# Branches A and B of a gated decoder block: GpSimd joins the turned halves, nine heads of A divide on VectorE, the products with V stand later

## The chip, the cores and the metric

The kernel runs on one NeuronCore of a Trainium2 chip. A core has TensorE (PE, matrix products into PSUM), VectorE (DVE), ScalarE (ACT), GpSimd (POOL) and SyncE (SP, which here only issues DMAs). Each engine works through its own queue in order; semaphores hold an instruction until what it reads or overwrites is ready. The metric is device time of one execution in microseconds (us). The profile adds a record of one execution: start and length of every instruction, and the clock that TensorE was granted.

## The reference

One decoder layer on 512 tokens of width 2048. A normed input is projected once and split over three token mixers, whose outputs are gated, projected, weighted and summed. Only the parts that the change touches are shown:

```python
def sliding_window_attention(...):          # branch A: 12 query heads, 4 key heads of 64
    scores = einsum('bnqkgd,bnskd->bnkgqs', qb, kb) * (d ** -0.5)
    scores = where(valid, scores + bias, NEG)            # ALiBi; each block sees itself and the one before
    m = maximum(max(scores, -1), sink)
    p = exp(scores - m)
    denom = sum(p, -1) + exp(sink - m)
    out = einsum('bnkgqs,bnskd->bnqkgd', p / denom, vb)

def forgetting_attention(...):              # branch B: 12 heads of 64
    sc = einsum('bqhd,bshd->bhqs', qb, k) * scale + cq - ck     # causal
    out = einsum('bhqs,bshd->bqhd', softmax(where(mask, sc, NEG)), v)

def hybrid_layer(...):
    proj = rms_norm(x) @ w_in
    ua = (ya * silu(za)) @ w_branch_a;  ub = ...;  uc = ...
    y = g[0] * ua + g[1] * ub + g[2] * uc
    return x + y @ w_out
```

All inputs are 32-bit floats.

## The kernel before

A 32-bit number enters TensorE as two parts: a rounded one (`hi`, an ACT copy) and the rest (`lo`, a DVE subtraction). Each large product is three: hi by hi, hi by lo, lo by hi.

**The main stream.** The input projection runs as chunks: `qB0, kB0, vB0, qB1, kB1, vB1, qA0, qA1, kvA, z0, mem, qC, z1, z2, z3`. A chunk is eight units (`mem`: sixteen smaller ones); a unit loads two 128-row slices of the weights (SP), splits them (ACT line 212, DVE line 215) and multiplies (PE line 301). A unit is 24 main products on PE (`mem`: 12): 384 columns wide in the B and A chunks, 512 from `kvA` on. After a chunk's last unit four PSUM banks are emptied (line 446 for queries and keys, lines 464 and 466 for values). After `z3` come the gate logits, branch products and output product; the change touches nothing there.

**The order of the work.** All of it is written by hand. A clock counts main products: three of them are half a step unit (`tick`), so a *step unit* below is six main products. Each attention head is a `Chain`: a base time and a list of steps with offsets (`STEPS_B`, `STEPS_A`), and named counters that hold a step back until a buffer is free in the planned order. At each tick the steps that are due are written into the engines' queues between the main products. So the step numbers say where an instruction stands in its queue, not when it runs. Branch B's heads 0 to 5 run under `qB1, kB1, vB1`, heads 6 to 11 under `qA0, qA1, kvA`; branch A's twelve heads run under `z0, mem, qC`; branch C's after them.

**One head of B** (A alike, with other offsets and sizes): GpSimd makes the bias (lines 625, 626); PE makes the scores of four 128-query blocks (589, 590); DVE adds the bias and finds the maximum (613); ACT takes the exponential and its sum (616); DVE inverts the sum (593) and the block is divided by it (594: on DVE for B, on GpSimd for A). The probabilities must then be turned, keys on the partitions. That goes by DMA in 16-bit halves:

- *halves* (636, 638; A: 724, 726, 728): GpSimd sorts the upper and lower 16 bits of each number apart, into `s1`;
- *send* (643; A: 734): SP issues one transposing DMA, `s1` to `s2`;
- *join* (649; A: 739): the halves are put together again into 32-bit numbers, `pt`. 2560 16-bit elements per partition in B, 1792 in A; read in order, written with a gap;
- *hi* (655; A: 745) on ACT, then *lo* (658; A: 748) on DVE;
- *products with V* (667; A: 757): eight on PE, which alternate between hi and lo; then ACT and DVE copy the result out (579, 583).

`PH`, `PL`, `pt`, `s1` and `s2` exist once each, so each waits for its last reader.

`STEPS_B[10..14]` are send, join, hi, lo, products; `STEPS_A[4], [5], [6], [10], [11]` the same for A. `scaled` (line 592) holds the reciprocal and the division.

Of the kernel before, what the change touches and what calls it, by code (L numbers as in the profile page):

```python
# [31 lines left out]
UK = 2  # L32
BOFF = (0, 512, 1024, 896)

BASES_B = ((14, 26, 38, 46, 58, 70), (14, 26, 38, 46, 58, 70))
BASES_A = (10, 18, 26, 34, 42, 50, 62, 69, 76, 83, 90, 97)
BASES_C = (12.0, 19.5, 28.0, 33.5)
STEPS_B = (-12, -8.5, -2, -1.5, 0, 1, 1.0, 1.5, 3.5, 5, 10.5, 16.5, 18, 19, 20.5, 4.5)
STEPS_A = (-5.0, -1.0, -0.5, -1.5, 6.5, 10.5, 11.5, -6.5, 3, 3.5, 12.5, 13.5)
STEPS_C = (-8, -3.5, 0.5, 1, 8.0, 4.5, 10)  # L40

PREP_Q = ((-1.5, 22.0, 43.5), (2.5, 22.0, 43.5))
# [8 lines left out]
EXP_B, EXP_A, EXP_C, DIV_B, DIV_A, DIV_C = (1.0, 0.5, 1.0, 3, 3.5, 3.0)  # L51
# [6 lines left out]
def tile_hybrid_block(ctx, tc, xT, x, memT, mem, ng, mng, w_in, b_forget, gqa, gka, sinks, gqb, gkb, gqc, gkc,  # L58
                      w_mem, w_a, w_b, w_c, w_out, relm, out):
    nc = tc.nc  # L60
    ve, ac, po, pe, sy = nc.vector, nc.scalar, nc.gpsimd, nc.tensor, nc.sync
# [7 lines left out]
    def f32(ap):  # L69
        return ap.bitcast(F32)  # L70
# [68 lines left out]
    def at_slot(t, f):  # L139

        heapq.heappush(agenda, (t, next(seq), f))

    def later(dt, f):
        at_slot(clock[0] + dt, f)
# [246 lines left out]
    def u16(ap):  # L391
        return ap.bitcast(U16)
# [142 lines left out]
    def sbank(name):  # L535
        return bank(1, name)
# [55 lines left out]
    def scaled(p, den, i, engine=po):  # L592
        ve.reciprocal(den[:, 4 + i:5 + i], den[:, i:i + 1])  # L593
        engine.tensor_scalar(p, p, den[:, 4 + i:5 + i], None, op0=ALU.mult)  # L594

    def head_B(h, kv):

        s = {}

        def s1(i):  # L600
            q, kh, kl, v, hv, cb = kv()
            if i == 0:
                s["p"] = at.p.tile([P, 1280], F32, tag="P", bufs=2, name=f"pB{h}")
                s["den"] = cp.tile([P, 16], F32, tag="den", bufs=2, name=f"denB{h}")
            p, den = s["p"], s["den"]
            o = (0, 128, 384, 768)[i]
            n = (i + 1) * P
            bi = s["b", i]
            sb = sbank(f"sB{h}_{i}")
            scores(sb[:, :n], q, kh, kl, i, slice(0, n))  # L610
            pi = p[:, o:o + n]
            nm = den[:, 8 + i:9 + i]
            ve.tensor_tensor_reduce(out=pi, in0=sb[:, :n], in1=bi[:, :n], scale=-1.0, scalar=3.0e38,  # L613
                                    op0=ALU.add, op1=ALU.min, accum_out=nm)
            release("bias")
            later(EXP_B, lambda: ac.activation(pi, pi, AF.Exp, bias=nm, scale=-1.0, accum_out=den[:, i:i + 1]))  # L616
            later(DIV_B, lambda: scaled(pi, den, i, ve))
            s["p", i] = pi
            if i > 1:
                later(DIV_B + 0.5, lambda: halves(i))  # L620

        def sb(i):
            n = (i + 1) * P
            bi = at.p.tile([P, S], F32, tag="bias", bufs=2, name=f"biB{h}_{i}")
            po.tensor_scalar(bi[:, :n], kv()[5][:, :n], -1.0, cq[:, i, h:h + 1], op0=ALU.mult, op1=ALU.add)
            po.affine_select(out=bi[:, i * P:n], in_=bi[:, i * P:n], pattern=[[-1, P]], compare_op=ALU.is_ge,
                             fill=NEG, base=0, channel_multiplier=1)
            s["b", i] = bi

        def halves(i):  # L630

            if i == 0:
                s["s1"] = spare(0, f"s1B{h}", U16, 2560).rearrange("p (e j n) -> p e j n", e=2, n=P)
            src = u16(s["p", i]).rearrange("p (j n e) -> p e j n", n=P, e=2)
            n = min(i + 1, 3)
            po.tensor_copy(s["s1"][:, :, i:i + 3 * n - 2:3, :], src[:, :, :n, :])
            if i == 3:
                po.tensor_copy(s["s1"][:, :, 7:8, :], src[:, :, 3:4, :])
                release("P")

        def send():
            s["s2"] = spare(1, f"s2B{h}", U16, 2560)
            sy.dma_start_transpose(out=s["s2"].rearrange("p (x n) -> p x n", n=P),
                                   in_=s["s1"].rearrange("p e j n -> p (e j n)"))
            release("S1")

        def join():
            s["t"] = spare(2, f"ptB{h}")
            ac.copy(u16(s["t"]).rearrange("p (n e) -> p e n", e=2), s["s2"].rearrange("p (e n) -> p e n", e=2))
            release("S2")  # L650

        def s2():
            s["hi"] = at.p.tile([P, 1280], F32R, tag="PH", bufs=1, name=f"phB{h}")
            s["lo"] = at.p.tile([P, 1280], F32R, tag="PL", bufs=1, name=f"plB{h}")
            ac.copy(s["hi"], s["t"])

        def s2l():
            ve.tensor_tensor(s["lo"], s["t"], f32(s["hi"]), op=ALU.subtract)
            release("RW")

        def s3():
            q, kh, kl, v, hv, cb = kv()
            av = avbank(f"avB{h}")
            for j in range(NT):
                n = S - j * P
                for w, t in enumerate((s["hi"], s["lo"])):
                    pe.matmul(av[:, j * P:], v[hv // 4][:, j, hv % 4, :], t[:, BOFF[j]:BOFF[j] + n],
                              start=(j == 0 and w == 0), stop=(j == NT - 1 and w == 1))
            pv_out(av, ysv("B", h // 2)[(h % 2) * 64:(h % 2) * 64 + 64, :], h % 2, f"avsB{h}", PV_B)

        def done():
            release("Q", "KH", "KL", *(["cb"] if h % 2 else []))

        o = STEPS_B
        steps = [(o[2], ["bias"], lambda: sb(0)), (o[3], ["bias"], lambda: sb(1)), (o[4], ["P"], lambda: s1(0)),
                 (o[5], [], lambda: s1(1)), (o[6], ["bias"], lambda: sb(2)), (o[7], ["bias"], lambda: sb(3)),
                 (o[8], [], lambda: s1(2)), (o[15], ["S1"], lambda: (halves(0), later(0.5, lambda: halves(1)))), (o[9], [], lambda: (s1(3), done())),
                 (o[10], ["S2"], send), (o[11], ["RW"], join), (o[12], ["PT"], s2), (o[13], [], s2l),
                 (o[14], ["T"], lambda: (s3(), release("PT")))]
        return steps  # L680
# [3 lines left out]
    def head_A(h, kv):  # L684
        s = {}
# [5 lines left out]
        def s1(pr):  # L691
            q, kh, kl, v, hv = kv()
            if pr == 0:
                p = at.p.tile([P, 1280], F32, tag="P", bufs=2, name=f"pA{h}")
                s["den"] = cp.tile([P, 16], F32, tag="den", bufs=2, name=f"denA{h}")
                s["p"] = p[:, :1028].rearrange("p (i k) -> p i k", k=257)
                ve.tensor_copy(s["p"][:, :, 256:257], nsink[:, h:h + 1].unsqueeze(1).to_broadcast([P, NT, 1]))
            bi, den, pv = s["bi"], s["den"], s["p"]
            sb = sbank(f"sA{h}_{pr}").rearrange("p (i k) -> p i k", k=256)
            for i in (2 * pr, 2 * pr + 1):  # L700
                c = P if i == 0 else 0
                scores(sb[:, i % 2, c:], q, kh, kl, i, slice(i * P - P + c, i * P + P))
            for i in (2 * pr, 2 * pr + 1):
                c = P if i == 0 else 0
                nm = den[:, 8 + i:9 + i]
                ve.tensor_tensor_reduce(out=pv[:, i, c:256], in0=sb[:, i % 2, c:], in1=bi[:, c:256], scale=-1.0,
                                        scalar=nsink[:, h:h + 1], op0=ALU.add, op1=ALU.min, accum_out=nm)
                later(EXP_A, lambda i=i, c=c, nm=nm: ac.activation(
                    pv[:, i, c:257], pv[:, i, c:257], AF.Exp, bias=nm, scale=-1.0, accum_out=den[:, i:i + 1]))
                later(DIV_A, lambda i=i, c=c: scaled(pv[:, i, c:256], den, i))  # L710

        def spot(n, name):
            if h < 6:
# [22 lines left out]

        def join():
            s["t"] = tokp.tile([P, 1024], F32, tag="V2", bufs=1, name=f"ptA{h}")[:, :896]
            ac.copy(u16(s["t"]).rearrange("p (n e) -> p e n", e=2), s["s2"].rearrange("p (e n) -> p e n", e=2))  # L739
            release("S2")  # L740

        def s2():
# [19 lines left out]

        o = STEPS_A
        return [(o[7], ["bias"], sb), (o[2], ["P"], lambda: s1(0)), (o[3], [], lambda: (s1(1), done())),
# [64 lines left out]
    def heads_B(part):  # L829
# [15 lines left out]
        def mk(hl):  # L845
            def kv():
                q, k = cache[hl // 2, "q"][hl % 2], cache[hl // 2, "k"][hl % 2]
                return q, k[0], k[1], toks[f"vB{part}"], hl, cache[hl // 2, "c"][:, hl % 2, :]
            base = BASES_B[part][hl]
            pre = [(PREP_Q[part][hl // 2] - base, ["T", "Q", "Q", "cb"], lambda: prep(hl // 2, "q")),  # L850
# [752 lines left out]
    for e in range(2):  # L1603
        kt = at.p.tile([P, S], F32R, name=f"kl{e}", tag=f"kl{e}")
        po.memset(f32(kt[64:128, :]), 0.0)
        klt.append(kt)
    plan(BASES_B[0], heads_B(0))
    run(n_p1, n_p2)
    plan(BASES_B[1], heads_B(1))
    run(n_p2, n_p3)  # L1610
# [56 lines left out]
```

## Time and profile before

| what | value |
|---|---|
| device time, median of 3 runs | 1576.67 us (1573.59 to 1577.78) |
| the profiled execution | 1580.97 us, its span 1579.2 us |
| PE busy | 1499.9 us, 95% |
| DVE / ACT / POOL busy | 1101.5 / 786.1 / 244.6 us |
| granted TensorE clock, mean | 0.971 |
| join in B (ACT line 649) | 12 of 3105 ns |
| join in A (ACT line 739) | 12 of 2234 ns |

How to read it: times in the trace count from the span's start. The *waits* view adds up, per pair, how long an engine sat idle and who ended it. The *windows* view gives each engine's busy time in a stretch, and the mean clock that TensorE was granted there (1.00 is full speed). A PE that is called busy can still be slow, when its clock is lowered. The *groups* view gives for instructions of one line and shape their number, total and mean time.

### The profile page before, as it was taken

What the parts mean: (1) busy time and instruction counts of PE and PEld (TensorE: products, weight loads), DVE (VectorE), ACT (ScalarE), POOL (GpSimd) and SP (SyncE); (2) the same over time, 40 slices, a digit from 0 to 9 for tenths busy, and PEclk for the clock granted to TensorE, in tenths of its full rate; (3) what the DMA queues carried; (4) which work ended last, traced back from release to release, by engine and by line L of the source; (5) the groups of instructions that cost most, each with busy time, mean ns of one, the idle gap of its engine ahead of it and who ended that gap; (6) DMA issues with size and microseconds to landing.
All of it is one profiled execution on the core that took longest, in us unless ns stands there. A gap on an engine that the chain in (4) does not pass through costs nothing.

```text
span 1579.2 us, 20058 instructions
## 1 busy us (share of the span) xinstructions
PE 1499.9 (95%) x6989; PEld 1282.7 (81%) x6989; DVE 1101.5 (70%) x1858; ACT 786.1 (50%) x1208; POOL 244.6 (15%) x319
## 2 busy tenths in 40 slices
PE   9998878888998799899999999999999999999998
PEld 9998878886776677788888888888888888888887
DVE  5475555556556565665888888887878566679997
ACT  5546555555455666654543544444444433346332
POOL 0123440344134345200000000000000021110000
PEclk9999889989998899999999999999999999999999
DMA  8773344434354443336776767676776877775774
GB/s 281 209 229 101 95 107 124 137 81 130 120 147 126 141 118 101 105 121 195 259 229 210 233 194 233 210 225 219 222 233 211 273 200 215 257 244 191 266 273 153
DMA packets 188622, 292.85 MB, mean 185 GB/s; under 512 B 75485, under 2 KB 115037, under 8 KB 188521
## 3 DMA queue, kind: packets, MB, share of 16 engines
q1 hardware_dynamic: 183480, 275.05, 56.7%
q10 hardware_dynamic: 5040, 16.53, 3.1%
q8 instruction: 55, 0.90, 0.2%
q14 instruction: 47, 0.38, 0.1%
HBM read 244.58 MB, written 31.48 MB: 175 GB/s over the span
## 4 chain that ended last, share of the span: by engine, by line
PE 59%; DMA 2%; ACT 2%; DVE 1%; issue 1%; POOL 1%; ACTq 0%; DVEq 0%; POOLq 0%; SPq 0%
PE P L1140 38%; PE z L301 8%; PE uA L1140 4%; PE uB L1140 3%; PE uC L1140 3%; PE qC L301 1%; DMA s2A<-s1A 1%; POOL pA L594 1%; DMA gates<-R 1%; DMA gB<-gates 0%; PE avA L757 0%; PE avC L810 0%; ACT wb L212 0%; ACT ptA L739 0%; DMA wa<-in_w_mem_dram 0%
## 5 line engine op out<-in xcount | busy, mean ns | idle before, releaser
L215 DVE TENSOR_TENSOR wc<-wa,wb 128x512 fp32r<-128x512 f32 (+2 forms) x252 | 152.1, 641 | 134.8 <-ACT wb L212 126.6
L212 ACT CAST wb<-wa 128x512 fp32r<-128x512 f32 (+2 forms) x252 | 130.4, 566 | 134.2 <-PE z L301 27.7
L1182 ACT CAST wa<-rawl 128x1024 fp32r<-128x1024 f32 x85 | 89.4, 1052 | 207.4 <-DVE rawl L1072 149.9
L1072 DVE TENSOR_TENSOR rawl<-rawl 128x512 f32<-128x512 f32 x256 | 177.0, 692 | 6.8 <-DMA rawl<-in_w_out_dram 2.4
L1456 POOL TENSOR_TENSOR y<-y,gA 128x512 f32<-128x512 f32 x16 | 28.1, 1792 | 733.8 <-DVE gA L1454 733.8
L1185 DVE TENSOR_TENSOR wc<-rawl,wa 128x1024 fp32r<-128x1024 f32 x85 | 104.9, 1235 | 51.6 <-ACT wa L1182 50.0
L1185 DVE TENSOR_TENSOR we<-rawl,wd 128x512 fp32r<-128x512 f32 (+1 forms) x128 | 122.2, 954 | 4.5 <-ACT wd L1182 0.9
L1182 ACT CAST wd<-rawl 128x512 fp32r<-128x512 f32 (+1 forms) x128 | 106.8, 834 | 24.5 <-DVE rawl L1072 21.0
L301 PE MATMUL z<-ah,wb 128*128 128x512 f32 x256 | 103.2, 403 | 1.5 <-DVE V_vA L466 1.5
L301 PE MATMUL z<-al,wb 128*128 128x512 f32 x256 | 101.0, 395 | 0.0
L301 PE MATMUL z<-ah,wc 128*128 128x512 f32 x256 | 101.0, 394 | 0.0
L1182 ACT CAST wb<-rawl 128x1024 fp32r<-128x1024 f32 x43 | 45.3, 1053 | 87.6 <-DVE rawl L1072 67.5
L1140 PE MATMUL P<-wd,xlx 128*128 128x512 f32 x192 | 74.7, 389 | 0.0
L1140 PE MATMUL P<-we,xhx 128*128 128x512 f32 x192 | 74.7, 389 | 0.0
L1140 PE MATMUL P<-wd,xhx 128*128 128x512 f32 x192 | 74.7, 389 | 0.0
L1185 DVE TENSOR_TENSOR wb<-rawl,wb 128x1024 fp32r<-128x1024 f32 x43 | 52.5, 1222 | 25.5 <-ACT wb L1182 25.3
L594 POOL TENSOR_SCALAR pA<-pA,denA 128x256 f32<-128x256 f32 (+1 forms) x48 | 45.8, 971 | 103.1 <-DVE denA L593 103.1
L1069 DVE TENSOR_TENSOR R<-P,R 128x512 f32<-128x512 f32 (+1 forms) x90 | 57.1, 674 | 6.1 <-PE P L1140 5.4
L301 PEld LDWEIGHTS z<-ah,wb 128*128 128x128 f32 x256 | 49.1, 192 | 11.4 <-DVE V_vA L466 1.9
L301 PEld LDWEIGHTS z<-ah,wc 128*128 128x128 f32 x256 | 48.8, 191 | 10.7
L301 PEld LDWEIGHTS z<-al,wb 128*128 128x128 f32 x256 | 49.0, 191 | 9.1
L616 ACT ACTIVATE pB<-pB,denB 128x128 f32<-128x128 f32 (+3 forms) x48 | 27.0, 562 | 57.0 <-DVE denB L613 56.9
(411 smaller groups left out, 4347.0 us busy)
## 6 DMA issues: line engine op xcount, KB each, us to landing
rawl<-in_w_in_dram SPq DMA_DIRECT2D x144, 512.0 KB, 4.4
rawl<-in_w_out_dram SPq DMA_DIRECT2D x48, 512.0 KB, 5.4
wa<-in_w_in_dram SPq DMA_DIRECT2D x62, 384.0 KB, 3.4
wa<-in_w_in_dram SPq DMA_DIRECT2D x64, 256.0 KB, 3.0
rawl<-in_w_in_dram SPq DMA_DIRECT2D x48, 256.0 KB, 4.1
gates<-R ACTq DMA_DIRECT2D x24, 512.0 KB, 7.7
wa<-in_w_in_dram SPq DMA_DIRECT2D x16, 512.0 KB, 3.7
wa<-in_w_mem_dram SPq DMA_DIRECT2D x16, 512.0 KB, 3.7
```

The lines of the kernel that those rows point to most:

```text
L212: ac.copy(hi[:, :n], raw[:, i, :n])
L215: ve.tensor_sub(lo[:, :n], raw[:, i, :n], f32(hi[:, :n]))
L301: pe.matmul(pb, a, m, start=b in fresh, stop=last and not todo[b])
L594: engine.tensor_scalar(p, p, den[:, 4 + i:5 + i], None, op0=ALU.mult)
L616: later(EXP_B, lambda: ac.activation(pi, pi, AF.Exp, bias=nm, scale=-1.0, accum_out=den[:, i:i + 1]))
L1069: ve.tensor_tensor(out, a, b, op=ALU.add)
L1072: ve.tensor_tensor(out, a, b, op=ALU.subtract)
L1140: pe.matmul(*args, **kw)
L1182: ac.copy(hi[:, :k, :], src)
L1185: return lambda: ve.tensor_tensor(lo[:, :k, :], src, f32(hi[:, :k, :]), op=ALU.subtract)
L1456: po.tensor_tensor(y, y, g, op=ALU.add)
```

## The change

Three things change, and the offsets with them.

- The join goes from ACT to GpSimd in all 24 heads.
- The division in A runs on DVE in nine heads (0 to 2 and 6 to 11) and stays on GpSimd in three (3 to 5).
- In the planned order of B the join stands 1 step unit earlier, hi 1 later, lo 1.5 later and the products with V 4.5 later; heads 4, 5, 10 and 11 begin 1 or 2 units earlier. In A the send stands 0.5 later, hi and lo 1 later, the products with V 3 later.

```diff
-BASES_B = ((14, 26, 38, 46, 58, 70), (14, 26, 38, 46, 58, 70))
+BASES_B = ((14, 26, 38, 46, 57, 68), (14, 26, 38, 46, 57, 68))
-STEPS_B = (-12, -8.5, -2, -1.5, 0, 1, 1.0, 1.5, 3.5, 5, 10.5, 16.5, 18, 19, 20.5, 4.5)
-STEPS_A = (-5.0, -1.0, -0.5, -1.5, 6.5, 10.5, 11.5, -6.5, 3, 3.5, 12.5, 13.5)
+STEPS_B = (-12, -8.5, -2, -1.5, 0, 1, 1.0, 1.5, 3.5, 5, 10.5, 15.5, 19, 20.5, 25, 4.5)
+STEPS_A = (-5.0, -1.0, -0.5, -1.5, 7, 10.5, 12.5, -6.5, 3, 3.5, 13.5, 16.5)
@@ head_B
         def join():
             s["t"] = spare(2, f"ptB{h}")
-            ac.copy(u16(s["t"]).rearrange("p (n e) -> p e n", e=2), s["s2"].rearrange("p (e n) -> p e n", e=2))
+            po.tensor_copy(u16(s["t"]).rearrange("p (n e) -> p e n", e=2), s["s2"].rearrange("p (e n) -> p e n", e=2))
@@ head_A
-                later(DIV_A, lambda i=i, c=c: scaled(pv[:, i, c:256], den, i))
+                later(DIV_A, lambda i=i, c=c: scaled(pv[:, i, c:256], den, i, po if 3 <= h < 6 else ve))
@@ head_A
         def join():
             s["t"] = tokp.tile([P, 1024], F32, tag="V2", bufs=1, name=f"ptA{h}")[:, :896]
-            ac.copy(u16(s["t"]).rearrange("p (n e) -> p e n", e=2), s["s2"].rearrange("p (e n) -> p e n", e=2))
+            po.tensor_copy(u16(s["t"]).rearrange("p (n e) -> p e n", e=2), s["s2"].rearrange("p (e n) -> p e n", e=2))
```

What that does to the queues is shown at three places. First, ACT around head 1 of B (`ptB1`, `phB1` are its joined and its hi tile, `wb35` the hi part of the weights of unit 35, `pB2` and `pB3` the next heads' probabilities, `avsB1` the copy that follows the products with V of head 1). Before:

```order
L649 COPY ptB1_1855<-s2B1_1759 128x2x1280
L551 ACTIVATE qB020_1878<-tqB02_1873,gs_qb_577 64x512
L551 ACTIVATE qB021_1880<-tqB02_1873,gs_qb_577 64x512
L616 ACTIVATE pB2_1783,denB2_1784<-pB2_1783,denB2_1784 128x512
L655 CAST phB1_1886<-ptB1_1855 128x1280
L212 CAST wb35_1894<-wa35_1826 128x384 x2
L616 ACTIVATE pB3_1927,denB3_1928<-pB3_1927,denB3_1928 128x128
L579 COPY avsB1_1963<-avB1_1938 64x512
```

And with the change:

```order
L616 ACTIVATE pB2_1771,denB2_1772<-pB2_1771,denB2_1772 128x512
L212 CAST wb35_1891<-wa35_1825 128x384 x2
L655 CAST phB1_1915<-ptB1_1841 128x1280
L616 ACTIVATE pB3_1926,denB3_1927<-pB3_1926,denB3_1927 128x128
L616 ACTIVATE pB3_1926,denB3_1927<-pB3_1926,denB3_1927 128x256
L212 CAST wb36_1963<-wa36_1895 128x384 x2
L616 ACTIVATE pB3_1926,denB3_1927<-pB3_1926,denB3_1927 128x384
L562 ACTIVATE kB020_2024<-tkB02_2019,g_kb_606 64x512
L565 ACTIVATE kB020_2024<-tkB02_2019,g_kb_606 64x512
L562 ACTIVATE kB021_2027<-tkB02_2019,g_kb_606 64x512
L565 ACTIVATE kB021_2027<-tkB02_2019,g_kb_606 64x512
L579 COPY avsB1_2033<-avB1_2003 64x512
```

The join has left the queue, hi stands behind the casts of unit 35 instead of ahead of them, and a whole further unit's casts (`wb36`) and the next pair's key preparation lie between hi and the copy that follows the products.

Second, GpSimd around heads 2 and 3 of B (`s1B3` holds head 3's halves, `biB4` head 4's bias). Before:

```order
L625 TENSOR_SCALAR biB3_3_1965<-cb01_1506,cq_100 128x512
L626 AFFINE_SELECT biB3_3_1965<-biB3_3_1965 128x128
L636 COPY s1B3_2008<-pB3_1927 128x2x128
L636 COPY s1B3_2008<-pB3_1927 128x2x2x128
L636 COPY s1B3_2008<-pB3_1927 128x2x3x128 x2
L638 COPY s1B3_2008<-pB3_1927 128x2x128
L625 TENSOR_SCALAR biB4_0_2083<-cb02_1870,cq_100 128x128
```

And with the change:

```order
L625 TENSOR_SCALAR biB3_3_1954<-cb01_1506,cq_100 128x512
L626 AFFINE_SELECT biB3_3_1954<-biB3_3_1954 128x128
L636 COPY s1B3_1997<-pB3_1926 128x2x128
L636 COPY s1B3_1997<-pB3_1926 128x2x2x128
L636 COPY s1B3_1997<-pB3_1926 128x2x3x128
L649 COPY ptB2_2058<-s2B2_1972 128x2x1280
L636 COPY s1B3_1997<-pB3_1926 128x2x3x128
L638 COPY s1B3_1997<-pB3_1926 128x2x128
L625 TENSOR_SCALAR biB4_0_2073<-cb02_1870,cq_100 128x128
```

Head 2's join now stands between the copies of head 3's halves, and ahead of head 4's bias.

Third, GpSimd around heads 7 and 8 of A (`pA7` are head 7's probabilities). Before:

```order
L594 TENSOR_SCALAR pA8_5431<-pA8_5431,denA8_5432 128x128
L594 TENSOR_SCALAR pA8_5431<-pA8_5431,denA8_5432 128x256 x3
L724 COPY s1A8_5503<-pA8_5431 128x2x128
L726 COPY s1A8_5503<-pA8_5431 128x2x256
L728 COPY s1A8_5503<-pA8_5431 128x2x512
```

And with the change:

```order
L689 TENSOR_SCALAR biA9_5474<-relt_90 128x256
L724 COPY s1A8_5502<-pA8_5420 128x2x128
L726 COPY s1A8_5502<-pA8_5420 128x2x256
L739 COPY ptA7_5508<-s2A7_5444 128x2x896
L728 COPY s1A8_5502<-pA8_5420 128x2x512
```

Four divisions have left GpSimd's queue for DVE's, and the join of the head before has come in among the halves.

## The prediction

> **What bounds the kernel now.** I read the page first, then the windows by stage, PE's waits, and one head in order of time.
>
> ```profile
> PE 1499.9 (95%) x6989; PEld 1282.7 (81%) x6989; DVE 1101.5 (70%) x1858; ACT 786.1 (50%) x1208; POOL 244.6 (15%) x319
> ...
> PEclk9999889989998899999999999999999999999999
> ```
>
> PE is the bound at 95%, but the clock row dips just where the heads of B and A run. The windows cut there (columns: stretch, length, PE, PEld, DVE, ACT, POOL busy, PE's clock, DMA):
>
> ```profile
> 120.00:430.00 310.00, 267.17 (x1340) 245.41 (x1338) 176.36 (x425) 172.17 (x305) 103.85 (x169) 0.91 0.42 113
> 445.00:662.00 217.00, 188.88 (x850) 154.04 (x849) 131.57 (x323) 137.46 (x265) 90.78 (x104) 0.91 0.45 122
> 662.00:840.00 178.00, 178.00 (x825) 148.08 (x824) 127.77 (x182) 84.21 (x132) 0.00 (x0) 1.00 0.59 190
> 840.00:1579.00 739.00, 733.90 (x3252) 607.21 (x3250) 581.24 (x729) 322.29 (x371) 28.15 (x16) 1.00 0.70 226
> ```
>
> From 662 on PE neither idles nor slows; nothing is to be won there. In B's stretch it idles 310 - 267.2 = 42.8 us, in A's 28.1. The clock of 0.91 costs at most 0.09 x (310 + 217) = 47 us more; some of the slow time lies inside the idle time, so I take 40. About 110 us is all that a better order of the heads can give. PE's waits say what it idles for (total, times, longest):
>
> ```profile
> PE avB L667 <- DVE plB L658: 24.5, 11, 2.8
> PE avA L757 <- DVE plA L748: 15.7, 10, 3.7
> PE avB L667 <- ACT phB L655: 8.6, 6, 2.7
> PE avA L757 <- ACT phA L745: 8.5, 7, 3.3
> PE kB L301 <- ACT t_qB L446: 3.1, 2, 2.5
> PE qA L301 <- ACT t_qA L446: 3.1, 2, 2.5
> ```
>
> 57.3 of the 71 us are the products with V, waiting for hi and lo: PE gets to them too early. Head 7 of B in order of time (start, length, what, idle before):
>
> ```profile
> 326.95 3.10 ACT L649 COPY ptB<-s2B 128x2560 uint16<-128x2560 uint16 x1
> ...
> 332.59 1.24 ACT L655 CAST phB<-ptB 128x1280 fp32r<-128x1280 f32 x1
> ...
> 334.27 1.03 DVE L215 TENSOR_TENSOR wc<-wa,wb 128x384 fp32r<-128x384 f32 x2 [0.89 <-ACT wb L212]
> 335.22 1.49 DVE L658 TENSOR_TENSOR plB<-ptB,phB 128x1280 fp32r<-128x1280 f32 x1
> ...
> 333.88 0.49 PE L667 MATMUL avB<-phB,V_vB 128*128 128x512 f32 x1 [2.58 <-ACT phB L655]
> 336.76 0.79 PE L667 MATMUL avB<-plB,V_vB 128*128 128x512 f32 x1 [2.38 <-DVE plB L658]
> ```
>
> PE reaches the products at 333.88 - 2.58 = 331.3, while ACT is still in the work that its 3.1 us join pushed back. lo ends at 336.7: 5.5 us late. The clock follows these waits:
>
> ```profile
> 319.00:331.00 12.00, 12.00 (x74) 11.86 (x72) 7.48 (x23) 6.85 (x12) 4.79 (x9) 1.00 0.25 68
> 331.00:343.00 12.00, 7.04 (x25) 6.34 (x24) 6.94 (x19) 6.34 (x15) 6.73 (x11) 0.72 0.36 87
> 343.00:355.00 12.00, 11.88 (x70) 11.43 (x69) 7.39 (x18) 8.41 (x12) 4.33 (x7) 1.00 0.20 47
> ```
>
> **The change, part by part.** *Length of a step unit without waits.* B's stretch holds 1340 PE instructions in some 310 - 42.8 - 24 = 243 us, 0.18 us each. A unit has six main products, and each head adds 16 (half of a pair's 8 transposes comes on top), 12 heads over 192 units: 7.2 instructions, 1.3 us. A's has 850 in 172 us and 8.3 to a unit: 1.65 us.
>
> *The products with V stand later.* Head 7 was 5.5 us late. The join leaves ACT (-3.1), lo stands 1.5 units later (+2.0), the products 4.5 (-5.9): lo is ready 1.5 us before PE asks. The average head of B waited 33.1/12 = 2.8 and comes out 4 us early. Head 10 of A, among the worst:
>
> ```profile
> 642.38 0.38 PE L757 MATMUL avA<-phA,V_vA 128*128 128x256 f32 x1 [3.29 <-ACT phA L745]
> 643.51 0.58 PE L757 MATMUL avA<-plA,V_vA 128*128 128x256 f32 x1 [0.74 <-DVE plA L748]
> ```
>
> PE was there at 642.38 - 3.29 = 639.1 and got lo at 643.5, 4.4 us late: 4.4 - 2.2 (join) + 1.65 (lo later) - 3 x 1.65 = -1.1, so 1.1 us early; the average of A (24.2/12 = 2.0) is 3.5 early. So nearly all 57.3 us go; I leave 6 for heads whose queues run late: **-51**.
>
> *The join leaves ACT.* The 3.1 us waits at the ends of `qB1` and `qA0` came of it as well:
>
> ```profile
> 145.62 3.10 ACT L649 COPY ptB<-s2B 128x2560 uint16<-128x2560 uint16 x1
> 148.60 0.56 ACT L446 ACTIVATE t_qB<-qB,rstds 128x384 f32<-128x384 f32 x1
> ```
>
> The emptying of PSUM stood behind head 0's join, and `kB` waited for the banks. With 3.1 us gone from in front, both waits go: **-6**. The other small waits (9 us) I leave.
>
> *The clock.* In the three rows above it fell with these waits; with them gone 40 us shrink to some 7: **-33**.
>
> *The join on GpSimd.* No row shows GpSimd writing 16-bit numbers with gaps. The nearest are its halves, the same numbers read with gaps, and the join on ACT:
>
> ```profile
> L636 POOL COPY s1B<-pB 128x768 uint16<-128x768 uint16 x24 | 20.9, 872 | 67.9 <-DVE pB L594 67.9
> L638 POOL COPY s1B<-pB 128x256 uint16<-128x256 uint16 x12 | 5.6, 464 | 0.0
> L649 ACT COPY ptB<-s2B 128x2560 uint16<-128x2560 uint16 x12 | 37.3, 3105 | 0.0
> L1456 POOL TENSOR_TENSOR y<-y,gA 128x512 f32<-128x512 f32 x16 | 28.1, 1792 | 733.8 <-DVE gA L1454 733.8
> ```
>
> (872 - 464)/512 = 0.8 ns an element gives 2.3 us for 2560 as the lower end; GpSimd's dearest row, 1792/512 = 3.5 ns, gives 9.0 (A: 6.3) as the upper. A gain beside the ACT join is in the first, a loss in the second. I take 2.6 us (A: 1.9), nearest the halves, which are the same copy backwards. hi stands 3.5 units = 4.6 us behind the join in B, 2 units = 3.3 us in A, so ACT doesn't wait. GpSimd's load in B becomes (103.9 + 31)/243 = 55%. Behind the join stand the next head's halves and bias: head 3's last halves come up to 2.6 us later, and with them its send. The send lands within 5 us, its join stands 5 units = 6.5 us behind (A: 3.5 units = 5.8):
>
> ```profile
> DMA to landing us min/median/max: 4.1/4.1/4.9
> ...
> DMA to landing us min/median/max: 3.4/3.5/5.3
> ```
>
> (B's transposing DMA, then A's.) SP itself issues the same DMAs in nearly the same places. If that cover is gone, GpSimd waits for the landing, and head 3's hi with it.
>
> *Nine divisions on DVE.* 36 instructions:
>
> ```profile
> L594 POOL TENSOR_SCALAR pA<-pA,denA 128x256 f32<-128x256 f32 x36 | 36.6, 1033 | 0.0
> L594 DVE TENSOR_SCALAR pC<-pC,denC 128x256 f32<-128x256 f32 x16 | 5.7, 354 | 0.6
> ```
>
> GpSimd loses some 35 us in A's stretch and gains 12 x 1.9 = 23. DVE gains about 36 x 0.35 = 12.4: (131.6 + 12.4)/172 = 84% without waits, in queue order. At 840 to 1579 it was 79% busy and PE lost nothing, so this is hidden by the units' distance between split and use; without that cover it would cost at most its 12.4.
>
> *A new wait.* Head 5's products now come just after the first bank of `vB1` is full, and emptying that bank (ACT, line 464) overwrites the V tile that they read. ACT waits about 1.1 us there, with the other three banks behind it; PE wants the first bank back 18 products (3.1 us) later. Hidden.
>
> *GpSimd beside DVE.* DVE's subtractions from two tiles run longer where GpSimd works:
>
> ```profile
> L748 DVE TENSOR_TENSOR plA<-ptA,phA 128x896 fp32r<-128x896 f32 x12 | 14.7, 1224 | 5.6 <-ACT phA L745 5.5
> ...
> L1185 DVE TENSOR_TENSOR wc<-rawl,wa 128x1024 fp32r<-128x1024 f32 x59 | 72.1, 1222 | 42.2 <-ACT wa L1182 40.7 <-PE z L301 1.4
> L1185 DVE TENSOR_TENSOR we<-rawl,wd 128x512 fp32r<-128x512 f32 x40 | 27.4, 685 | 0.0
> ```
>
> At 760 to 1200, with GpSimd idle, (1222 - 685)/512 = 1.05 ns an element; 896 elements should take 1.09 us and take 1.22 in A. A stretch of 0.13 us on average is small; with longer GpSimd copies and a fuller DVE I add **+8** of new waits.
>
> Sum: -51 - 6 - 33 + 8 = -82. The profiled execution took 1581.0, so it would take 1499; the median of the runs shown is 4.3 lower: **1495 us**.
>
> **The rivals.**
>
> *DVE is held by the joins* (faster, but by half). A DVE instruction that reads two tiles and meets a join would stand until it ends, up to 2.6 us. B's worst head has 1.5 us in hand and would be 1.1 late; the weights' subtractions (line 215) are met too. At 1.5 us per head 36 us of waits come back, and 10 of clock: 1495 + 46 = 1541. For it: the stretch above. Against: it is 0.13 us so far, with GpSimd busy 42% of A's stretch. The Trainium skill, "SBUF — State Buffer", section "Who interferes with whom", speaks for it: a VectorE instruction with two SBUF inputs and a GpSimd instruction that reads SBUF exclude each other for the whole length of the first. The trace agrees in kind, by those 0.13 us.
>
> *The clock doesn't follow the waits* (faster by less): the 33 us stay, 1528. Against: the three rows at 319 to 355. The Trainium skill, "TensorE: Matmul & The Clock Gate", section "HAM oscillation — how this bites in real kernels", asks only that no idle gap exceed some 3.4 us; read strictly, waits of 2 to 3 us would not lower the clock, and the loss would have another cause. Here it fell to 0.72 with two waits of 2.6 and 2.4 us close together, so the row goes against that reading.
>
> *GpSimd becomes the bound* (slower). At the 3.5 ns end the join takes 9.0 us in B, 6.3 in A; ACT stands at hi 4.4 and 3.0 us per head, with the casts of the weights behind it: 12 x 7.4 = 89 us of waits in place of 57, the clock no better, less the 6: 1577 + 32 - 6 = 1603. It decides from the point where 24 waits equal the old 57: about 7.4 us a join in B. Against: all of GpSimd's 16-bit copies run at 0.8 to 1.1 ns an element.
>
> **How the numbers follow.** My forecast 0.72, DVE held 0.10, the clock's loss staying 0.06, GpSimd as the bound 0.09, all effects cancelling 0.03. The forecast's own range is 1468 (all 110 us won) to 1525. The range over all reaches up past the second rival, to 1550; slower cases and no change, 0.12, are left out. Within 0.3%, about 5 us, a measurement can't tell a change from none. Faster 0.72 + 0.10 + 0.06 = 0.88, same 0.03, slower 0.09.
>
> **What would show it.** Right: the four rows of PE's waits at lines 667 and 757 sum to under 10 us; the windows over the B and A heads show 0.98 or more; the `t_qB` and `t_qA` waits are gone; the join reads 2.3 to 2.8 us (A: 1.6 to 2.1) on POOL. Wrong: ACT waits for POOL at lines 655 and 745 (join too slow); lines 658, 748 and 215 on DVE run much longer than now (DVE held); waits gone with the clock still at 0.91; PE's idle time moved to lines 589 or 301, for DVE.

## The result and the profile after

The changed kernel takes **1520.4 us** (median; 1519.8 to 1521.1), the kernel before 1575.7 beside it: a ratio of 0.965, 95% interval 0.963 to 0.967. It is faster by 55 us. The prediction was 1495, with a range of 1468 to 1550: the direction was right, and 25 us of the expected gain are missing. The profiled execution took 1520.6 us with a span of 1518.6.

The head of the page after:

```profile
PE 1473.9 (97%) x6989; PEld 1258.7 (83%) x6989; DVE 1164.8 (77%) x1894; ACT 724.5 (48%) x1184; POOL 304.9 (20%) x307
```

DVE is busy 63 us longer than before (1101.5). The divisions of A that moved to DVE take 13.9 of that (the prediction: 12.4); the other 49 us are the subject of this study. The stages again, in windows (stretch, length, PE, PEld, DVE, ACT, POOL, PE's clock, DMA); PE's last products with V of B now stand at 383 and those of A at 604, where it was 420 and 660 before, so the windows are cut at 410 and 640:

```profile
120.00:410.00 290.00, 268.87 (x1434) 247.11 (x1433) 227.48 (x470) 146.66 (x315) 170.72 (x190) 0.98 0.48 130
410.00:640.00 230.00, 213.15 (x1017) 172.30 (x1016) 181.51 (x391) 127.93 (x287) 89.34 (x76) 0.96 0.44 124
```

PE idles 21.1 + 16.9 = 38 us in these windows where it idled 42.8 + 28.1 = 71 in those before, and the clock in these stages rose from 0.91 to 0.98 and 0.96. By the prediction's measure of it (the missing share of the clock times the length) the slow clock costs at most 0.02 x 290 + 0.04 x 230 = 15 us in place of 47. What PE still idles for, in its waits after:

```profile
PE kB L301 <- DVE wc L215: 4.9, 4, 2.2
PE mem L301 <- ACT wb L212: 4.8, 2, 3.5
PE mem L301 <- DVE wc L215: 4.5, 5, 2.5
PE kB L301 <- ACT t_qB L446: 2.5, 1, 2.5
PE qA L301 <- ACT t_qA L446: 2.5, 1, 2.5
PE kvA L301 <- DVE wc L215: 2.4, 1, 2.4
...
PE vB L301 <- DVE wc L215: 1.9, 1, 1.9
PE qA L301 <- DVE wc L215: 1.8, 2, 0.9
...
PE avA L757 <- DVE plA L748: 0.5, 1, 0.5
...
PE avB L667 <- DVE plB L658: 0.3, 1, 0.3
```

The products with V (lines 667 and 757) wait 0.8 us where they waited 57.3. In their place stands `wc`, the low half of the weights, which DVE makes by subtraction on line 215: 4.9 + 4.5 + 2.4 + 1.9 + 1.8 = 15.5 us. Before, that was one row:

```profile
PE mem L301 <- DVE wc L215: 1.2, 2, 0.9
```

Why DVE is late with it can be seen in the groups of the two kernels, first before, then after (total, mean ns):

```profile
L215 DVE TENSOR_TENSOR wc<-wa,wb 128x512 fp32r<-128x512 f32 (+2 forms) x252 | 152.1, 641 | 134.8 <-ACT wb L212 126.6 <-DMA g_qb<-in_gqb_dram 4.5 <-DMA mngt<-in_mng_dram 3.3
```

```profile
L215 DVE TENSOR_TENSOR wc<-wa,wb 128x512 fp32r<-128x512 f32 (+2 forms) x252 | 186.6, 779 | 80.5 <-ACT wb L212 79.9
L649 POOL COPY ptB<-s2B 128x2560 uint16<-128x2560 uint16 x12 | 38.3, 3191 | 8.6 <-DVE x3s L1069 4.3 <-DMA s2B<-s1B 4.3
L739 POOL COPY ptA<-s2A 128x1792 uint16<-128x1792 uint16 x12 | 27.9, 2321 | 17.9 <-DMA s2A<-s1A 10.4 <-DVE plA L748 7.5
```

The same 252 subtractions take 34.5 us more. And the join takes 3.19 us in B and 2.32 in A on GpSimd: no less than on ScalarE (3.105 and 2.234), and above the 2.6 and 1.9 of the prediction. One place of the trace after, in order of time, shows what the two have to do with each other:

```profile
329.54 3.17 POOL L649 COPY ptB<-s2B 128x2560 uint16<-128x2560 uint16 x1
329.66 4.34 DVE L215 TENSOR_TENSOR wc<-wa,wb 128x512 fp32r<-128x512 f32 x2
```

The two subtractions need 0.68 us each. The first began 0.1 us behind the join and took 3.54 us (the longest of line 215 in this kernel); it ended at 333.2, half a microsecond after the join's end at 332.7, as if it had stood still until GpSimd had finished. At another place DVE works beside one join for its whole length:

```profile
168.77 3.12 POOL L649 COPY ptB<-s2B 128x2560 uint16<-128x2560 uint16 x1
...
169.47 0.68 DVE L583 TENSOR_TENSOR ysB<-avB,avsB 64x512 f32<-64x512 f32 x1
...
170.25 1.86 DVE L594 TENSOR_SCALAR pB<-pB,denB 128x384 f32<-128x384 f32 x1
...
173.69 1.23 DVE L215 TENSOR_TENSOR wc<-wa,wb 128x384 fp32r<-128x384 f32 x2
...
174.30 0.51 PE L301 MATMUL kB<-wc,ah 128*128 128x384 f32 x1 [2.15 <-DVE wc L215]
```

Line 583 adds a tile of SBUF to a PSUM bank (`avB`) and takes its usual 0.68 us in the middle of the join. Line 594, a division (median 0.42 us), takes 1.86 and ends 0.2 us after the join; then DVE is late with `wc`, and PE idles 2.15 us.

Counted over the whole trace after (duration of each DVE instruction that overlaps a join, less the shortest of its form), DVE loses 46 us in all. 21 subtractions of line 215 overlap a join and lose 29.6 us; of line 422, which also reads two SBUF tiles, 4 do and lose 7.7. Lines 563, 583, 613, 706 and 886, which read PSUM, overlap joins too, 19 times, and lose 0.2 us together. The loss follows a simple rule: of lines 215 and 422, 19 instructions began inside a join, and each lost what was left of the join at its start, less 0.17 to 0.19 us.

### The profile page after: what moved, and what is told of

It reads as the page before. It is cut to its first block, busy times and chain, and to the rows that moved or that the text cites. A ratio compares the mean times of both kernels' runs of the same rounds, so it can differ in the third digit from the quotient of the medians.

```text
span 1518.6 us, 20051 instructions
## 1 busy us (share of the span) xinstructions
PE 1473.9 (97%) x6989; PEld 1258.7 (83%) x6989; DVE 1164.8 (77%) x1894; ACT 724.5 (48%) x1184; POOL 304.9 (20%) x307
## 4 chain that ended last, share of the span: by engine, by line
PE 61%; DVE 1%; issue 0%; DVEq 0%
PE P L1140 40%; PE z L301 8%; PE uA L1140 4%; PE uB L1140 4%; PE uC L1140 3%; PE avC L810 0%; DVE wc L215 0%; PE ptC L799 0%; PE yt L1503 0%; PE sC L783 0%; DVE pA L594 0%; PE sC L784 0%; PE sC L782 0%; DVE ysB L1000 0%; PE tqC L544 0%; DVE t_qC L422 0%
## 5 line engine op out<-in xcount | busy, mean ns | idle before, releaser
L215 DVE TENSOR_TENSOR wc<-wa,wb 128x512 fp32r<-128x512 f32 (+2 forms) x252 | 186.6, 779 | 80.5 <-ACT wb L212 79.9
L1182 ACT CAST wa<-rawl 128x1024 fp32r<-128x1024 f32 x85 | 89.5, 1053 | 207.6 <-DVE rawl L1072 162.1
L301 PE MATMUL mem<-wb,mhl 128*128 128x512 f32 x128 | 46.1, 424 | 6.5 <-ACT wb L212 4.8
```

The source lines that it names most:

```text
L215: ve.tensor_sub(lo[:, :n], raw[:, i, :n], f32(hi[:, :n]))
L301: pe.matmul(pb, a, m, start=b in fresh, stop=last and not todo[b])
L1182: ac.copy(hi[:, :k, :], src)
```

## The experiments

Two theories stood at the start. **H** (hold): a GpSimd join holds the DVE instruction that meets it until the join ends; this is the prediction's first rival. **F** (full): no hold matters; DVE is late because its queue got longer and the steps stand elsewhere.

### Both joins back on ScalarE

```diff
 (changed kernel, lines 649 and 739)
-po.tensor_copy(u16(s["t"])..., s["s2"]...)
+ac.copy(u16(s["t"])..., s["s2"]...)
```

> The changed kernel with both joins back on ScalarE; offsets and divisions stay as changed. Theory H (the GpSimd join holds DVE: a DVE instruction that meets it stands until it ends): line 215 falls from 779 to about 660 ns on average and its longest from 3.5 to under 1.6 us, PE's waits for wc (line 215) fall from 15.7 to under 5 us; ACT's queue is 3.1 us per head longer, which the later products mostly cover (PV waits 3 to 8 us) and which brings back the 3.1 us waits for t_qB and t_qA. Time about 1510 us (1500 to 1517). Theory F (no hold matters; DVE is simply full, in queue order, at the quicker pace): waits for wc stay near 15 us and the 64 us that go back to ACT only cost: 1528 to 1540 us.

Measured: **1497.9 us** (1497.5 to 1498.6), ratio 0.951, interval 0.949 to 0.952. Moving the joins to GpSimd cost 22.5 us. That is even below the range of H, which allowed the products with V 3 to 8 us of waits: they do not wait here either, no row of lines 667 and 757 is left. The longest subtraction of line 215 is 1.52 us again, and PE's waits for `wc` are 4.6 us. The row that matters, and the windows:

```profile
L215 DVE TENSOR_TENSOR wc<-wa,wb 128x512 fp32r<-128x512 f32 (+2 forms) x252 | 158.3, 667 | 87.9 <-ACT wb L212 79.5 <-DMA g_qb<-in_gqb_dram 4.5 <-DMA mngt<-in_mng_dram 3.3
```

```profile
120.00:410.00 290.00, 278.40 (x1498) 255.97 (x1497) 206.60 (x493) 187.92 (x341) 130.58 (x181) 0.99 0.49 135
410.00:640.00 230.00, 217.68 (x1062) 177.58 (x1061) 169.40 (x391) 154.63 (x305) 55.03 (x61) 0.98 0.46 135
```

In B's window PE does 64 more matmuls than after the change, and DVE more instructions in less busy time (493 in 206.6 us against 470 in 227.5). F is out as the main cause: DVE has as many instructions in both kernels (1894), and the edit leaves their order alone.

### The products with V later, and nothing else

```diff
 (kernel before)
-BASES_B ... 58, 70        +BASES_B ... 57, 68
-STEPS_B ... 18, 19, 20.5, 4.5     (o[14]: products)
+STEPS_B ... 18, 19, 25, 4.5
-STEPS_A ... 12.5, 13.5            (o[11]: products)
+STEPS_A ... 12.5, 16.5
```

(Two of B's bases change with them.)

> The kernel before with the products with V alone later (25 in B, 16.5 in A, with the bases that go with it); joins on ACT, divisions of A on GpSimd, hi, lo and send where they were. Theory H: the products' 57 us of waits go (to under 8), the clock follows, the other 14 us of waits stay: 1576 - 50 - 30 = 1496 to 1512 us, so the moved join was worth nothing or cost time. Theory F: the join had to leave ACT to make hi and lo early enough; 20 us or more of the products' waits remain, and the time is 1525 to 1545 us.

Measured: 1518.0 us (1515.7 to 1520.5), ratio 0.964, interval 0.962 to 0.965; between the two expectations. This small part alone brings as much as the whole change. The waits of the products are gone, but others came, and one of them shows why the steps in front were moved too. ScalarE, and then PE, in this kernel:

```profile
169.80 3.11 ACT L649 COPY ptB<-s2B 128x2560 uint16<-128x2560 uint16 x1
...
175.06 1.24 ACT L655 CAST phB<-ptB 128x1280 fp32r<-128x1280 f32 x1
176.21 0.92 ACT L212 CAST wb<-wa 128x384 fp32r<-128x384 f32 x2
...
176.77 0.63 PE L301 MATMUL kB<-wb,ah 128*128 128x384 f32 x1 [3.83 <-ACT wb L212]
```

The cast of the weights stood behind the join and hi together, and PE idled 3.8 us for it.

### The changed kernel, each GpSimd join cut in four

```diff
-po.tensor_copy(<the whole join>)
+for c in range(0, 1280, 320):      # A: range(0, 896, 224)
+    po.tensor_copy(d[:, :, c:c + 320], e[:, :, c:c + 320])
```

> The changed kernel with each GpSimd join cut into four instructions of a quarter of the length (the same elements). Theory H (held for a whole GpSimd instruction): DVE gets in between the quarters; the longest line 215 falls from 3.5 to about 1.5 us, its average from 779 towards 700 ns, waits for wc from 15.7 to about 8 us; time 1508 to 1515 us. Theory F: nothing changes but 72 more instructions on GpSimd: 1519 to 1527 us.

Measured: 1510.2 us (1508.8 to 1511.2), ratio 0.959, interval 0.957 to 0.960. GpSimd now spends more on the joins, 47.6 + 41.9 = 89.5 us instead of 66.2, and the kernel is 10 us faster:

```profile
L651 POOL COPY ptB<-s2B 128x640 uint16<-128x640 uint16 x48 | 47.6, 1057 | 9.5 <-DVE x3s L1073 4.4 <-DMA s2B<-s1B 4.3 <-DVE wc L215 0.8
L743 POOL COPY ptA<-s2A 128x448 uint16<-128x448 uint16 x48 | 41.9, 939 | 18.2 <-DMA s2A<-s1A 11.3 <-DVE plA L752 4.9 <-DVE denA L708 2.0
```

The longest subtraction of line 215 falls from 3.54 to 1.52 us, and what DVE loses beside the joins, counted as above, from 46 to 25 us. So it is the length of the single instruction that counts, not GpSimd's busy time. PE's waits for `wc` fall from 15.7 to 12.0 us, where H expected about 8, and 12 of the 22.5 us remain.

### All of A's divisions on GpSimd

```diff
-scaled(pv[:, i, c:256], den, i, po if 3 <= h < 6 else ve)
+scaled(pv[:, i, c:256], den, i)
```

> The changed kernel with all twelve heads of A dividing on GpSimd, as before. Theory H: DVE loses 12.4 us of work in A's stretch but 36 more GpSimd instructions of about 1 us stand beside it and ahead of the halves and joins; A's heads come later: 1520 to 1530 us. Theory F (DVE is full in A): DVE's relief shows, waits for wc in the mem chunk fall: 1510 to 1517 us.

Measured: 1526.7 us (1523.0 to 1527.2), ratio 0.969, interval 0.967 to 0.970. The nine heads' divisions on VectorE were worth 6 us: with all twelve heads' on GpSimd, whose queue also has the joins, A's products wait again, 5.7 us in all.

### The join on GpSimd in one branch only

> The changed kernel with A's join back on ScalarE and B's left on GpSimd. Theory H (a GpSimd join holds the VectorE instruction that meets it; with both joins on ScalarE the kernel took 1497.9 us, with both on GpSimd 1520.4): the cost of 22.5 us is shared by the time that the joins take (12 x 3.2 in B, 12 x 2.3 in A), so some 13 us belong to B: 1508 to 1514. If instead the cost were in A alone, where GpSimd also divides three heads: 1497 to 1501. If it were in B alone: 1518 to 1521.

> The changed kernel with B's join back on ScalarE and A's left on GpSimd. H: some 9 of the 22.5 us belong to A: 1504 to 1510. Cost in A alone: 1518 to 1521; in B alone: 1497 to 1501. If the two branches are independent, this and the kernel with B's join alone on GpSimd should together lose 22.5 us against the 1497.9 of both on ScalarE.

(The edit of the first run, in one of the two lines.) Measured: B alone **1511.9 us** (1507.4 to 1513.2), A alone **1505.7** (1504.2 to 1507.7); ratios 0.959 (0.957 to 0.961) and 0.955 (0.953 to 0.957). Against 1497.9 that is +14.1 and +7.9, together 22.0 of the 22.5: the branches add up. Per microsecond of joining the cost is 14.1/38.3 = 0.37 in B and 7.9/27.9 = 0.28 in A. In B, PE's idle time between 120 and 410 rises by 9.2 us against the kernel with ScalarE joins, and its waits for `wc` there by 9.0: the low halves of the weights are nearly all of it. In A it rises by 6.4 us between 410 and 640, and the waits for `wc` of `mem` by only 1.8; the rest is spread over waits for ACT and other DVE lines.

### The kernel before, with the joins on GpSimd alone

> The kernel before with both joins on GpSimd and nothing else changed (the products with V stay early, all heads of A divide on GpSimd). H: the products' waits of 57 us shrink where ScalarE's queue was late (3.1 us less in front of hi in B, 2.2 in A), but the VectorE holds cost 20 to 25 us and the subtraction that makes lo is held too: 1565 to 1590, no clear gain. F (no hold, the move merely relieves ScalarE): about 30 us of the waits and some clock go, 1535 to 1550.

(Lines 649 and 739 of the kernel before: `po.tensor_copy` for `ac.copy`.) Measured: **1588.2 us** (1586.6 to 1591.3), ratio 1.008, interval 1.006 to 1.010. By itself this part of the change is a loss of 12 us, small but clear of the interval. The products' waits, with nothing moved later, do not shrink; their sum is 66.4 us where it was 57.3:

```profile
PE avB L667 <- DVE plB L658: 25.2, 11, 2.8
PE avA L757 <- ACT phA L745: 14.4, 3, 5.8
PE avA L757 <- DVE plA L748: 13.4, 10, 2.4
PE avB L667 <- ACT phB L655: 13.4, 8, 3.6
```

### Where the rest of the later steps' gain is

The changed kernel with ScalarE joins and all divisions on GpSimd has, against the kernel before, only later steps:

> The changed kernel with both joins on ScalarE and all twelve heads of A dividing on GpSimd: it differs from the kernel before by the later steps alone (hi, lo, sends and products). It tells what the 20 us are between the kernel before with only the products later (1518.0) and the changed kernel with ScalarE joins (1497.9): if the nine divisions on VectorE give them, about 1515 to 1518; if the later hi, lo and join order gives them, about 1500 to 1504 (the divisions are then worth the 6 us or less that they were worth beside the GpSimd joins).

Measured: 1498.5 us (1497.6 to 1499.8), ratio 0.951, interval 0.949 to 0.952, just below the second of the two expectations. The divisions' place is worth nothing here; the 20 us between 1518.0 and 1498 come from the offsets of join, hi, lo and send. Then B's offsets alone, on top of the later products:

```diff
-STEPS_B ... 16.5, 18, 19, 25, 4.5
+STEPS_B ... 15.5, 19, 20.5, 25, 4.5      (join, hi, lo, products)
```

> The kernel before with only the products with V later (1518.0 us) plus the changed steps of B: join one unit earlier, hi one and lo one and a half units later. A's steps stay as before. The step from 1518.0 to 1498.5 (all changed steps, all divisions on GpSimd) is then shared out: if the steps of B carry it (VectorE and ScalarE no longer get hi and lo in the same places as the weights' casts), 1500 to 1507; if those of A carry it, 1513 to 1518; in shares of the stages' idle time (B had the larger part), about 1506 to 1512.

Measured: **1500.6 us** (1499.3 to 1501.9), ratio 0.952, interval 0.951 to 0.954. B's three numbers give 17 of the 20 us. ScalarE at the place shown above:

```profile
166.31 3.13 ACT L649 COPY ptB<-s2B 128x2560 uint16<-128x2560 uint16 x1
...
172.16 0.91 ACT L212 CAST wb<-wa 128x384 fp32r<-128x384 f32 x2
172.97 1.26 ACT L655 CAST phB<-ptB 128x1280 fp32r<-128x1280 f32 x1
```

With the join a unit earlier and hi a unit later, the weights' cast stands between them, no longer behind both. PE's waits for this cast in `kB` and `qA` fall from 6.8 to 2.5 us. These 4.3 us are one part of the 17; other waits went as well, among them 3.3 us of score products that waited for the maxima of line 613.

### The hold by itself: a dead copy, and a dead fill

So far GpSimd's joins could also have cost time because their result comes late. Two kernels separate this for B: the joins stay on ScalarE, and beside each join of B GpSimd does work that nobody reads, into a free tile. The dead copy reads SBUF and writes it; the fill only writes.

```diff
 (both joins on ScalarE; in B's join)
+po.tensor_copy(dum.rearrange("p (n e) -> p e n", e=2),
+               u16(rstdb).unsqueeze(1).to_broadcast([P, 2, 1024]))
 or
+po.memset(dum.rearrange("p (n e) -> p e n", e=2), 0)
```

> The changed kernel with both joins on ScalarE (1497.9 us) plus, beside each join of B, a GpSimd copy of 2048 16-bit numbers with gaps in the output, from a constant into a tile that nobody reads. Nothing waits for it, and it delays no step that PE needs but through GpSimd's queue. H (the hold alone costs): at 1.2 ns an element it takes 2.4 us; B's real joins took 3.2 us and cost 14 us in all, so about 10 us come: 1504 to 1512, with the longest subtraction of the weights on VectorE over 2.2 us where it was 1.5. If instead the joins cost time because their result came late on GpSimd (hi and lo late): 1496 to 1500 and no longer VectorE instruction.

> As the kernel with the dead copy beside each join of B, but GpSimd only fills the tile with a constant: the same output, nothing read. If a GpSimd instruction has to read SBUF to hold VectorE: 1496 to 1500, and the longest subtraction of the weights stays at 1.5 us. If writing is enough: a cost in proportion to the length of the fill, 1503 to 1512 at 2 to 2.4 us, and subtractions over 2 us.

Measured: the copy **1508.7 us** (1506.4 to 1513.4), ratio 0.958 (0.956 to 0.960); the fill **1503.2** (1503.1 to 1504.4), ratio 0.954 (0.953 to 0.956). The GpSimd groups and DVE's, first with the copy, then with the fill:

```profile
L653 POOL COPY dum<-rstdb 128x2048 uint16<-128x2048 uint16 x12 | 33.0, 2749 | 0.0
...
L215 DVE TENSOR_TENSOR wc<-wa,wb 128x512 fp32r<-128x512 f32 (+2 forms) x252 | 175.2, 734 | 79.8 <-ACT wb L212 74.7 <-DMA g_qb<-in_gqb_dram 4.5
L595 DVE TENSOR_SCALAR pB<-pB,denB 128x128 f32<-128x128 f32 (+3 forms) x48 | 20.7, 432 | 1.7
```

```profile
L653 POOL MEMSET dum<- 128x2048 uint16 x12 | 29.5, 2456 | 0.0
...
L215 DVE TENSOR_TENSOR wc<-wa,wb 128x512 fp32r<-128x512 f32 (+2 forms) x252 | 157.7, 664 | 84.7 <-ACT wb L212 84.2
L595 DVE TENSOR_SCALAR pB<-pB,denB 128x128 f32<-128x128 f32 (+3 forms) x48 | 26.2, 546 | 1.7
```

Without either, line 215 had a mean of 667 ns. The copy, on which nothing depends, lengthens it to 734 (16.9 us over the 252) and costs 10.9 us of time: 0.33 us per microsecond of copying, where B's real joins cost 0.37. So per microsecond of copying the cost is nearly that of the joins, without any late result. (The dead copy's four runs spread over 7 us, more than other kernels' do.) The fill leaves line 215 at 664, though 16 of its subtractions overlap a fill. It holds another kind: B's divisions (one tile in, one out) go from 403 to 546 ns, the longest to 2.8 us. This, and GpSimd's queue behind the fill, cost 5.3 us; how these two share it the runs do not say. So the fill's time came as the second expectation had it, but not by way of the subtractions.

The fill also bounds what else the dead copy could have cost. Both lengthen GpSimd's queue by nearly the same time (33.0 and 29.5 us), so by the fill's 5.3 us about half of the copy's 10.9 at most can come from that queue; that leaves the rest to the held subtractions. No dead copy was run beside A's joins. There ScalarE waits 10.7 us for the join in the kernel with A's joins alone on GpSimd, so for A's 7.9 us the hold and the late result are not told apart.

The Trainium skill, "SBUF — State Buffer", section "Who interferes with whom", has this rule: a VectorE instruction with two inputs in SBUF contends with a GpSimd instruction that reads SBUF and not with one that only writes, and a single-input operation such as a scaling by a scalar contends where it runs in a two-port mode. The trace agrees where it can be seen: subtractions 734 ns beside the copy and 664 beside the fill, divisions 546 beside the fill, line 583 with its PSUM input 0.68 us inside a join. Which mode an instruction runs in, no trace here shows.

### All divisions on VectorE, both joins on ScalarE

```diff
 (both joins on ScalarE)
-scaled(pv[:, i, c:256], den, i, po if 3 <= h < 6 else ve)
+scaled(pv[:, i, c:256], den, i, ve)
```

> The changed kernel with both joins on ScalarE and all twelve heads of A dividing on VectorE. With all on GpSimd it was 1498.5 and with nine on VectorE 1497.9, so the divisions' place should not matter: 1495 to 1500. If GpSimd's last three heads are what delays the send of A (6.2 us in front of the weights' DMAs near 455 us, and 4.6 us of waits on PE behind them): 1490 to 1494.

Measured: **1495.5 us** (1494.7 to 1496.1), ratio 0.949, interval 0.948 to 0.951. It beats both kernels, by 80 us the one before and by 25 the changed one. Against 1497.9 the 2.4 us are near what can be told apart. The 4.0 us in which PE waited for the weights' casts of `mem` are no longer among its larger waits, but 4.6 us for their low halves are, so the gain that the second expectation hoped for did not come; the time lies in the range of the first.

## Why the prediction was right, and where it was wrong

**What bounds the kernel** held: the gain came out of PE's idle time and out of the clock in the stages of B and A. Between the two profiled executions the span falls by 60.6 us (1579.2 to 1518.6). 34.6 of these are idle time of PE; the other 26.0 are its busy time (1499.9 to 1473.9), with the same 6989 instructions, so they are the clock.

**The products with V stand later, -51:** right. Their waits went from 57.3 to 0.8 us, 56.5 won. But the working leaned on the join leaving ScalarE (3.1 of 5.5 us in head 7), and the runs show that this was not needed: with the joins still on ScalarE no such wait is left.

**The join leaves ACT, -6:** wrong. The waits for `t_qB` and `t_qA` went from 3.1 to 2.5 us each, 1.2 in all. The prediction saw a join directly in front of the emptying and took it for the whole cause. But the 3.1 us were two waits, 0.6 for the third bank, behind the join, and 2.5 for the fourth. Between these two emptyings stand four activations that prepare the keys (0.68 us each, lines 562 and 565), before as well as after. And on GpSimd the join delays the third bank in another way, as the trace after shows:

```profile
142.47 3.87 DVE L215 TENSOR_TENSOR wc<-wa,wb 128x384 fp32r<-128x384 f32 x2 [0.70 <-ACT wb L212]
142.57 3.42 POOL L649 COPY ptB<-s2B 128x2560 uint16<-128x2560 uint16 x1
...
146.85 0.62 ACT L616 ACTIVATE pB<-pB,denB 128x384 f32<-128x384 f32 x1 [1.96 <-DVE denB L613]
...
147.47 0.57 ACT L446 ACTIVATE t_qB<-qB,rstds 128x384 f32<-128x384 f32 x1
147.93 0.67 ACT L562 ACTIVATE kB<-tkB,g_kb 64x512 fp32r<-64x512 f32 x1
...
150.71 0.58 ACT L446 ACTIVATE t_qB<-qB,rstds 128x384 f32<-128x384 f32 x1
```

The join holds a subtraction, the maximum behind it comes late, and ACT waits 1.96 us for it right in front of the third emptying. With the joins cut in four the two waits are 1.4 us each, with ScalarE joins 2.5, with the products alone later 3.1. So some of the 6 us was there to be had, but not with a long join on GpSimd. Moving the four activations was not tried.

**The clock, -33:** the mechanism is right, the size 7 us too large (26.0 us of PE's busy time). The clock rose with the waits' end, from 0.91 to 0.98 and 0.96, and in the kernel with fewer waits (ScalarE joins) to 0.99 and 0.98; the bound fell from 47 to 15 us. Over the whole execution it was 0.971 before, 0.972 with the joins alone moved, where the products' waits stayed, and 0.994 with the products alone later, where they went. That speaks against the rival "the clock doesn't follow the waits".

**The join on GpSimd, 2.6 and 1.9 us:** too low, 3.19 and 2.32, though inside the bounds (2.3 to 9.0 in B). The remark that all of GpSimd's 16-bit copies run at 0.8 to 1.1 ns an element doesn't fit a row that the prediction itself shows, 464 ns for 256. ScalarE did wait for it, which was named as a wrong sign:

```profile
ACT phA L745 <- POOL ptA L739: 10.6, 4, 4.9
ACT phB L655 <- POOL ptB L649: 3.0, 2, 2.2
```

The products with V, late enough, didn't feel it; whether PE lost by it elsewhere in A is not shown. "GpSimd becomes the bound" stayed far off.

**Nine divisions on DVE, hidden:** right; beside the GpSimd joins they were a gain of 6 us, beside ScalarE joins worth nothing (1498.5 against 1497.9).

**A new wait, hidden:** right; after the change PE has no row of waits for the emptying of `vB` (line 466), where it had 0.7 us before.

**GpSimd beside DVE, +8:** this is the step that failed, in its size. PE's idle time fell by 34.6 us, while 56.5 + 1.2 = 57.7 were removed, so some 23 us of new waits came. Putting the joins back on ScalarE takes 14.3 us of idle time and 8.1 of busy time away again, and 22.5 us of the device time. The prediction read the stretch as a mean, 0.13 us, over the twelve instructions of line 748, and added a guess for longer copies. But only three of the twelve began inside a GpSimd copy, and they lost 0.19, 0.41 and 0.84 us. In the trace before, 21 DVE instructions of lines 215, 422 and 748 began inside a GpSimd copy, and each of them lost what was left of the copy, less 0.02 to 0.14 us. So a hold lasts as long as the copy does, and the price had to be read from the meetings and the copies' length, not from a mean. One place before already shows it:

```profile
521.82 1.49 DVE L748 TENSOR_TENSOR plA<-ptA,phA 128x896 fp32r<-128x896 f32 x1
522.31 1.89 POOL L728 COPY s1A<-pA 128x1024 uint16<-128x1024 uint16 x1
523.23 1.52 DVE L215 TENSOR_TENSOR wc<-wa,wb 128x512 fp32r<-128x512 f32 x1
```

The second subtraction needs 0.68 us alone; it took 1.52 and ended 0.55 us behind GpSimd's copy.

**The rival "DVE is held by the joins"** had the mechanism, at 0.10 and with 1541 us. It came out at half that price, 22.5 us and not 46: lo itself was ready in time nearly always (the products wait 0.8 us), and in B it was the weights' low halves that were late. The forecast's 1495 is about what the same change takes without its move to GpSimd (1497.9); that is luck, since the forecast counted this move as a gain.

**The signs.** Of the signs that it would be right one came in full (the products' waits, 0.8 us) and one in half (the clock: 0.98 in B, but 0.96 in A); the `t_qB` and `t_qA` waits are not gone, and the join is slower than it said. Three of the signs that it would be wrong came: ACT waits for POOL, line 215 runs longer, and PE's idle time moved to line 301, for DVE. The time still lies inside the forecast's own range of 1468 to 1525, but the change as a whole is what the later products alone bring (1518.0): the better order of hi and lo won 20 us more, and the joins on GpSimd gave them back.

## What to carry to other kernels

Before moving work to GpSimd, look in the trace at the longest, not the mean, DVE instructions that read two SBUF tiles, and at what GpSimd ran beside them: a hold can last until the moved instruction ends, so here a copy of 3 us was worse than four of 1 us, and worse than the same copy on a ScalarE that was half idle. Where a long copy stays on an in-order engine, put the cast that PE wants next between it and the following long step: three numbers, which do this among other things, were worth 17 us here. Take the parts of a change apart, too: its best part (the later products) hid that another was a loss of 22.5 us.

## What the runs showed of the hardware

- GpSimd wrote 16-bit numbers with gaps at 3191/2560 = 1.25 ns an element (in 640-element pieces 1057/640 = 1.65), ScalarE at 3105/2560 = 1.21. Taken as the prediction took the halves, by the difference of two lengths, it is (3191 - 1057)/1920 = 1.11 ns against 0.8 for the halves, which are read with gaps.
- A DVE instruction that reads two SBUF tiles and began inside a GpSimd copy lost what was left of the copy, less 0.02 to 0.19 us: 21 of 21 before, 19 of 19 beside the joins after; 0.68 us became 3.54. Instructions with an input in PSUM lost 0.2 us in 19 overlaps with joins.
- A GpSimd fill, which reads nothing, left these alone (664 against 667 ns) but held the scaling by a scalar (403 to 546 ns).
